# First groups of a hybrid streaming layer: six instead of four on unscaled tokens, operands renewed part by part, low parts on another engine, swish in pieces

## The chip, the cores and the metric

One core of a Trainium2 chip runs one layer of a hybrid trunk (a convolution group and a stick-breaking attention group side by side) on 2048 tokens and 16 meta tokens, in float32. The metric is the device time of one execution in microseconds. The page of the profile names the engines PE (TensorE), DVE (VectorE), ACT (ScalarE), POOL (GpSimd) and SP, which only starts transfers.

## The reference, cut to what matters

```python
u = rms_norm(h, pre_g)                       # per token: u = h * rate * g
proj = u @ w_in                              # 1024 -> 7 x 512 columns
glu_a, glu_b, conv_gate, q, k, v, sb_gate = split(proj)
c = glu_a * sigmoid(glu_b)
c = causal_depthwise_conv(c, conv_w, conv_b) # width 31
c = silu(layer_norm(c, conv_ln_g, conv_ln_b))
c = (c @ w_pw2 + b_pw2) * silu(conv_gate)
s = stick_breaking_attention(q, k, v) * silu(sb_gate)   # 8 heads x 64, strictly causal
h = h + rms_norm(concat[c, s] @ w_out, post_g)
```

The rate of a token is one number, so a product of unscaled tokens with the weights can be multiplied by the rate afterwards. The kernel uses that at its start: the rates take long to get, the products need not wait for them.

## The kernel before, in words

The 2048 tokens go in four chunks of 512 (chunk 0 carries the 16 meta tokens too). Each float32 operand is split into a high part (fp32r) and the rest, the low part: ACT copies the high part, DVE or POOL subtracts it, and each product of two such operands is three matmuls: high by high, high by low, low by high (`mm3`). The normed tokens of a chunk, transposed, are the tiles uh and ul (8 parts of 128 rows each); a weight is a slab of 128x512 numbers, loaded raw (wr), and its two parts lie in w. Two slabs make one group, the 128 output columns of one step of the input projection. Chunk 0 makes each group in two segments of 264 tokens, 24 matmuls each.

Chunk 0 begins with `load_first_in`: it brings the first 512 tokens transposed (ts, in tiles pr), splits them into uh and ul unscaled, and at once brings the same tokens in rows (tok), whose squares ACT sums; POOL makes the rates, PE turns them into a row (`spread`), and DVE scales ts by it (`times`). The groups of glu_b and glu_a (names G_B, G_A; `in_proj`) come first, in pairs j = 0 to 3. Before, pairs 0 and 1 ran on unscaled tokens, with `with_rates` putting the rates on their results; then `again` renewed uh and ul from the scaled ts, all eight parts in a row, and every later group ran on them.

Behind the pairs come the groups of k, v and q, then attention (`attention`) of the chunk, with which the gates, the norm of the convolution (`conv_norm`), the pointwise projection (`conv_out`) and the next chunk's projection are merged. The convolution of 31 taps per 128 channels runs on DVE as 31 operations that add into a bank cv; in chunk 0 all four tiles run there. `conv_norm` transposes the four tiles (acc), takes mean and variance per token, subtracts and multiplies rows that PE makes of them, and applies swish: per tile two operations of ACT and one product of DVE. `conv_parts` splits the result (mixs) for `conv_out`.

The order of all engines is written out by the program before it runs: `Clock` and `Engine` keep a forecast of each engine's time, `when` puts a deferred piece on a list with the operands it needs and a date before which it is not issued, `step` and `merge` pick what comes next. So a new date or a new cost moves instructions on all engines. What is issued stands in that order in each engine's queue, and the chip follows it. Weights pass through two raw buffers (RAWS) and four slabs of parts (WB); `load_raw` starts a load when a raw buffer is free. All instructions of an engine are issued from one line of the helper (L203 before, L206 after), so the profile tells them apart by tiles.

## Time and profile before

| | us |
|---|---|
| median of 3 runs (1358.3 to 1359.58) | 1358.92 |
| the profiled execution | 1360.08 |
| its span | 1357.9 |
| PE busy / DVE / ACT / POOL | 1320.4 / 1003.4 / 738.2 / 650.5 |
| TensorE's granted clock, mean | 0.988 |

In the rows a line reads: start, duration, engine, line of the program, operation, output <- inputs, shape, how many; in brackets the idle time of the engine ahead of it and what ended it. Tiles: T, mm, cv and av are banks of PSUM, all others lie in SBUF or, with wpack, xturn, x and the names on scr, in HBM. A busy PE isn't always at full speed: the granted clock (PEclk) is 1.00 or 0.50 in any short stretch of this profile.

### The profile page before, as it was taken

How to read it: one execution, taken by the hardware profiler on the slowest of the kernel's cores; microseconds unless marked ns; L12 is line 12 of the kernel's file. 1: busy time of each engine (PE TensorE's matmuls, PEld its weight loads, DVE VectorE, ACT ScalarE, POOL GpSimd, SP SyncE). 2: the span in 40 equal slices, each digit the busy share in tenths (PEclk: the TensorE clock that was granted, in tenths of full speed). 3: DMA queues.
4: the chain of work that ended last, by engine and by line, in shares of the span. 5: the costliest groups of instructions: out<-in, count | busy, mean ns of one | idle time of the engine just before them, and what ended most of it. 6: DMA issues, size and time to landing. Idle time of an engine off the chain costs nothing.

```text
span 1357.9 us, 21813 instructions
## 1 busy us (share of the span) xinstructions
PE 1320.4 (97%) x7584; PEld 1133.7 (83%) x7584; DVE 1003.4 (74%) x1417; ACT 738.2 (54%) x1459; POOL 650.5 (48%) x786
## 2 busy tenths in 40 slices
PE   7999989999998999999999999999999999999997
PEld 7898777887788987887779988888877899988797
DVE  4999864898984376995396468896557987898965
ACT  5334465344446545376645446488776657655542
POOL 5444668667466541297841143089886021141300
PEclk8999989999999999999999999999999999999999
DMA  6155968899985994676776597556777545586655
GB/s 223 66 155 179 343 228 291 295 311 319 336 284 176 305 355 139 195 238 214 230 252 185 168 295 263 176 176 216 221 223 240 174 136 179 161 279 215 210 155 179
DMA packets 163757, 304.95 MB, mean 225 GB/s; under 512 B 16688, under 2 KB 71152, under 8 KB 163648
## 3 DMA queue, kind: packets, MB, share of 16 engines
q1 hardware_dynamic: 149344, 253.49, 59.7%
q0 software_dynamic: 14304, 50.08, 9.4%
q8 instruction: 60, 0.98, 0.3%
q14 instruction: 49, 0.40, 0.1%
HBM read 221.85 MB, written 81.66 MB: 224 GB/s over the span
## 4 chain that ended last, share of the span: by engine, by line
PE 80%; DVE 7%; DMA 4%; ACT 3%; issue 3%; POOL 2%; SPq 0%; DVEq 0%; POOLq 0%; ACTq 0%
PE mm L203 51%; PE T L203 20%; PE av L203 8%; DVE cv L203 2%; DMA tok<-x 1%; DVE pr L203 1%; ACT ev L203 1%; DMA wr<-wpack 1%; POOL w L203 1%; DVE tok L203 1%; DVE ul L203 1%; DVE al L203 1%; POOL ev L203 1%; DVE acc L203 1%; DMA wscr<-w 1%
## 5 line engine op out<-in xcount | busy, mean ns | idle before, releaser
L203 PE MATMUL mm<-uh,w 128*128 128x512 f32 (+1 forms) x1664 | 517.9, 373 | 3.9 <-ACT uh L203 3.9
L203 PEld LDWEIGHTS mm<-uh,w 128*128 128x128 f32 x1664 | 302.2, 191 | 52.6 <-ACT uh L203 4.5
L203 DVE TENSOR_TENSOR al<-T,ah 128x512 fp32r<-128x512 f32 (+3 forms) x323 | 193.9, 600 | 164.7 <-ACT ah L203 163.1
L203 PE MATMUL mm<-ul,w 128*128 128x512 f32 (+1 forms) x832 | 307.0, 369 | 1.1 <-DVE ul L203 1.0
L203 DVE TENSOR_TENSOR_SCAN pr<-T,pr,zcol 128x512 f32<-128x512 f32 x192 | 245.0, 1276 | 47.9 <-ACT T L203 42.7
L203 ACT ACTIVATE ah<-T 128x512 fp32r<-128x512 f32 (+3 forms) x323 | 171.4, 531 | 141.9 <-PE T L203 140.4
L203 DVE SCALAR_TENSOR_TENSOR cv<-ct,cp,cv 128x512 f32<-128x512 f32 x319 | 239.2, 750 | 7.4
L203 ACT ACTIVATE T<-T 128x512 f32<-128x512 f32 (+2 forms) x320 | 167.4, 525 | 110.7 <-PE T L203 108.0
L203 POOL TENSOR_TENSOR acc<-acc,pd 128x512 f32<-128x512 f32 x150 | 194.2, 1294 | 44.5 <-ACT pd L203 37.4
L203 POOL TENSOR_TENSOR w<-wr,w 128x512 fp32r<-128x512 f32 x116 | 149.7, 1294 | 103.8 <-ACT w L203 101.0
L203 PE MATMUL T<-kk,q 128*128 128x512 f32 (+2 forms) x640 | 195.1, 387 | 3.0 <-DVE pr L203 2.3
L203 PEld LDWEIGHTS mm<-ul,w 128*128 128x128 f32 x832 | 158.6, 191 | 22.3 <-DVE ul L203 1.7
L203 PE MATMUL T<-ident,pr 128*128 128x128 f32 x1088 | 172.3, 274 | 1.0 <-DVE al L203 0.6
L203 PEld LDWEIGHTS T<-ident,pr 128*128 128x128 f32 x1088 | 133.9, 141 | 32.7 <-DVE pr L203 2.5
L203 DVE TENSOR_TENSOR_SCAN pr<-T,tri 128x128 f32<-128x128 f32 (+3 forms) x128 | 103.9, 815 | 31.9 <-ACT T L203 31.2
L203 PEld LDWEIGHTS T<-kk,q 128*128 128x128 f32 x640 | 106.4, 190 | 19.3 <-DVE pr L203 4.1
L203 PE MATMUL av<-ah,vk 128*128 128x512 f32 (+1 forms) x320 | 117.4, 367 | 0.0
L203 PE MATMUL av<-al,vk 128*128 128x512 f32 (+1 forms) x320 | 117.1, 366 | 0.0
L203 ACT ACTIVATE pd<-ct,cp 128x512 f32<-128x512 f32 x150 | 106.1, 718 | 19.0 <-POOL acc L203 18.1
L203 PE MATMUL mm<-uh,wr 128*128 128x512 f32 x320 | 115.2, 402 | 0.0
L203 ACT ACTIVATE w<-wr 128x512 fp32r<-128x512 f32 x116 | 72.1, 628 | 77.1 <-PE mm L203 35.2
L203 POOL COPY cm<-pr 128x1 f32<-128x1 f32 x120 | 23.7, 200 | 146.7 <-DVE pr L203 145.8
(188 smaller groups left out, 1802.2 us busy)
## 6 DMA issues: line engine op xcount, KB each, us to landing
w<-wscr SPq DMA_DIRECT2D x128, 512.0 KB, 4.1
wscr<-w POOLq DMA_DIRECT2D x76, 512.0 KB, 5.7
wr<-wscr SPq DMA_DIRECT2D x62, 512.0 KB, 4.2
wr<-wpack SPq DMA_DIRECT2D x58, 512.0 KB, 4.4
kk<-kscr SPq DMA_DIRECT2D x80, 256.0 KB, 4.9
vk<-vscr SPq DMA_DIRECT2D x80, 256.0 KB, 3.7
q<-qscr SPq DMA_DIRECT2D x64, 256.0 KB, 5.6
tok<-x SPq DMA_DIRECT2D x16, 512.0 KB, 8.2
```

What stands on the lines that cost most here:

```text
L203: return call(out, *args, **kw)
```

## The change

EARLY_PAIRS = 3: the first three pairs, six groups instead of four, run on unscaled tokens. The renewal of uh and ul is called by `mm3` behind each part's last product in the second segment of the sixth group (`then`), and the seventh group runs its two segments together in banks T, as the first group does. VectorE instead of GpSimd forms the low parts of slabs 0 and 2 to 7, and the raw loads behind these slabs have no date. The first weight load is cut in two, the second half behind the first part of the tokens; the meta tokens' transposed load moves ahead of the tokens; the last 256 tokens in rows are brought behind another weight load. A sigmoid at the very start brings its table in. The scalings of ts get dates, 1.5 us apart. PE's warm-up has 18 transposes instead of 20. In `conv_norm` of every chunk, the swish of tile j is a deferred piece with a date 1.5 us after that of tile j - 1.

```diff
@@ -66,6 +66,9 @@
         for k in range(0, KD, 2):
             yield "w_out", n, OC, k
+EARLY_PAIRS = 3
@@ -517,6 +520,7 @@
                 there.add(key)
             order.append((key, n, kept, save))
     todo_w = deque(order)
+    FIRST = [len(order) - i - 1 for i in (0, 2, 3, 4, 5, 6, 7)]
     whole = [key for key, n, kept, save in order if not kept]
     at = {key: i for i, key in enumerate(slab_keys())}
     todo_raw = deque(zip(whole[::2], whole[1::2]))
@@ -556,12 +560,19 @@
                         lambda: pool.dma_start(place[key], both.bitcast(F32)), [both[:, 1]]
                     )
-                split(raw[:, i], both[:, 0], both[:, 1], then=keep_it if save else None)
+                split(
+                    raw[:, i], both[:, 0], both[:, 1],
+                    dve if len(todo_w) in FIRST else pool,
+                    keep_it if save else None,
+                )
                 raws[0][1] += 1
                 if i:
                     raws.popleft()
                     when(
-                        lambda: load_raw(min(RAWS, len(raws) + 1)), [], date=pe.now + 2.0, tag="wr")
+                        lambda: load_raw(min(RAWS, len(raws) + 1)), [],
+                        date=0.0 if len(todo_w) in FIRST else pe.now + 2.0, tag="wr",
+                    )
             ready.append(
                 (key, [both[:, i].rearrange("p (k n) -> p k n", n=key[2]) for i in range(2)])
             )
@@ -582,7 +593,7 @@
             parts.append(both)
         return parts
-    def mm3(w, mh, ml, nk, cols, last=True, given=None, tag="mm"):
+    def mm3(w, mh, ml, nk, cols, last=True, given=None, tag="mm", then=None):
         pts = None
@@ -604,6 +615,8 @@
                     pe.matmul(pt, h, hi, start=(k == 0), stop=False)
                     pe.matmul(pt, h, lo, start=False, stop=False)
                     pe.matmul(pt, l, hi, start=False, stop=(k == nk - 1))
+                if then:
+                    then(k)
                 if last and (k % 4 == 3 or k == nk - 1):
                     release()
         return pts
@@ -623,8 +636,13 @@
         uh, ul = u_now
-        load_raw(1)
+        raw = T("wr", [P, 2, 4 * P], RAWS)
+        raws.append([raw, 0])
+        a, b = todo_raw.popleft()
+        sp.dma_start(raw[:, 0], wpack[at[a]])
         sp.dma_start(cp, cpack)
+        mt = T("pr", [P, KD, NM], PR)
+        sp.dma_start(mt, xturn[:, :, :NM])
         keep["turned", 0] = 0
         ts = []
         for k in range(KD):
@@ -632,8 +650,7 @@
             sp.dma_start(ts[k], xturn[:, k, NM:])
             when(lambda k=k: part_in(0, k, ts[k], uh, ul), [ts[k], cp])
             if k == 0:
-                mt = T("pr", [P, KD, NM], PR)
-                sp.dma_start(mt, xturn[:, :, :NM])
+                sp.dma_start(raw[:, 1], wpack[at[b]])
         def meta_in():
             hi, lo = uh[:, :, 0:NM], ul[:, :, 0:NM]
@@ -649,17 +666,23 @@
         when(meta_times, [mt, cp])
         load_raw()
-        todo = []
-        for i in range(NTB // 2):
+        measured = []
+        def fetch(i):
             t = tok()
             for b in range(2):
                 tb = 2 * i + b
                 sp.dma_start(t[:, b], x[tb * P : (tb + 1) * P, :])
-                todo.append((t[:, b], tb))
-        m = T("q2", [P, D], 2)[:NM]
-        sp.dma_start(m, meta)
-        todo.append((m, NTB))
-        measured = []
+                when(lambda b=b, tb=tb: measure(t[:, b], tb), [t[:, b]], tag="ev")
+        def fetch_meta():
+            m = T("q2", [P, D], 2)[:NM]
+            sp.dma_start(m, meta)
+            when(lambda: measure(m, NTB), [m], tag="ev")
+        fetch(0)
+        fetch_meta()
+        when(lambda: fetch(1), [], date=7.5)
         def measure(t, tb):
             n = t.shape[0]
@@ -668,11 +691,8 @@
                 junk[:n], t, AF.Square, scale=D ** -0.5, accum_out=squares[:n, tb : tb + 1]
             )
             measured.append(tb)
-            if len(measured) == len(todo):
+            if len(measured) == NTB + 1:
                 when(rates, [squares], [rate0])
-        for t, tb in todo:
-            when(lambda a=(t, tb): measure(*a), [t], tag="ev")
         def rates():
             pool.tensor_scalar(squares, squares, 1e-6, None, op0=ALU.add)
@@ -698,7 +718,9 @@
             for go in waiting:
                 go()
             for k in range(KD):
-                when(lambda k=k: times(k, pt), [ts[k], pt], [ts[k]])
+                when(
+                    lambda k=k: times(k, pt), [ts[k], pt], [ts[k]], date=pe.now + 3.0 + 1.5 * k
+                )
             dve.tensor_tensor(
                 mt, mt, row[:, :NM].unsqueeze(1).to_broadcast([P, KD, NM]), op=ALU.mult
             )
@@ -709,22 +731,21 @@
             dve.tensor_tensor(ts[k], ts[k], rates, op=ALU.mult)
             scaled.append(k)
-        def again():
-            yield need(given=lambda: len(scaled) == KD and "first" in keep)
-            keep["turned", 0] = 0
-            keep["normed"] = True
-            meta_in()
-            for k in range(KD):
-                when(lambda k=k: part_in(0, k, ts[k], uh, ul), [ts[k]])
-        return again()
+        def once_more(k):
+            if k == 0:
+                keep["turned", 0] = 0
+                when(meta_in, [mt], date=pe.now)
+            when(lambda: part_in(0, k, ts[k], uh, ul), [ts[k]], date=pe.now)
+        keep["scaled"] = lambda: "row" in keep and len(scaled) == KD
+        keep["once more"] = once_more
     def warm():
         pt = PT("T", [P, TC])
-        for _ in range(20):
+        for _ in range(18):
             pe.transpose(pt[:, :P], ident, ident)
     waiting = []
@@ -795,22 +816,24 @@
     def proj(c, g, evac, with_meta):
         yield need(given=lambda: ("turned", c) in keep and (c or "meta" in keep))
-        first = G_B, G_A, G_B + 1, G_A + 1
-        if c == 0 and g == first[-1]:
+        first = [n + j for j in range(EARLY_PAIRS) for n in (G_B, G_A)]
+        if c == 0 and g == first[3]:
             yield need(given=lambda: "row" in keep)
-        if c == 0 and g not in first:
-            keep["first"] = True
-            yield need(given=lambda: "normed" in keep)
         w = weights(w_in, g * P)
         uh, ul = u_now
         cols = segs(c, with_meta)
-        for part in [cols] if c == 0 and g == first[0] else [[a] for a in cols]:
+        for part in [cols] if c == 0 and g in (G_B, G_B + EARLY_PAIRS) else [[a] for a in cols]:
+            then = None
+            if c == 0 and g == first[-1] and part[-1] == cols[-1]:
+                yield need(given=keep["scaled"])
+                then = keep["once more"]
             pts = yield from mm3(
                 w, lambda k: uh[:, k], lambda k: ul[:, k], KD, part, part[-1] == cols[-1],
                 (lambda k: k < keep["turned", c]) if keep["turned", c] < KD else None,
-                "T" if c == 0 and g in first[1:3] else "mm",
+                "T" if c == 0 and g in (*first[1:3], G_B + EARLY_PAIRS) else "mm", then,
             )
             for pt, (o, n) in zip(pts, part):
                 evac(pt, o, n)
@@ -876,11 +899,11 @@
                 def go():
                     dve.tensor_tensor(t, pt, row[:, o : o + n], op=ALU.mult)
                     act.activation(t, t, AF.Sigmoid)
-                    if j < 2:
+                    if j < EARLY_PAIRS:
                         pool.tensor_tensor(t, t, row[:, o : o + n], op=ALU.mult)
-                if c == 0 and j < 2:
+                if c == 0 and j < EARLY_PAIRS:
                     with_rates(go)
                 else:
                     act.activation(t, pt, AF.Sigmoid)
@@ -1093,13 +1116,16 @@
                     lambda j=j, i=i: apply(j, i), [rows[i], accs[j]], [accs[j]]
                 )
         yield need(given=lambda: len(done) == 2 * NJ)
-        for j in range(NJ):
+        def swish(j):
             g, b = lng[:, j : j + 1], lnb[:, j : j + 1]
             sg, y = ev()[:, :TC], accs[j]
             act.activation(sg, y, AF.Sigmoid, scale=g, bias=b)
             act.activation(y, y, AF.Identity, scale=g, bias=b)
+            when(lambda: dve.tensor_tensor(y, y, sg, op=ALU.mult), [y, sg], [y])
+        for j in range(NJ):
             when(
-                lambda y=y, sg=sg: dve.tensor_tensor(y, y, sg, op=ALU.mult), [y, sg], [y]
+                lambda j=j: swish(j), [accs[j]], [accs[j]], date=pe.now + 1.5 * j, tag="ev"
             )
         keep["normed", c] = True
@@ -1802,10 +1828,12 @@
     ):
         new_u()
         warm()
-        once_more = load_first_in()
+        load_first_in()
+        act.activation(rate0[:, 0:1], zcol, AF.Sigmoid)
         prepare()
         clear()
-        spent = [merge(iter(()), either(in_proj(0), once_more), iter(()), [(1, 1)])]
+        spent = [merge(iter(()), in_proj(0), iter(()), [(1, 1)])]
         for half in range(2):
             in_us(4.0 + 6 * half, lambda half=half: load_in(1, half))
         for c in range(NCH):
```

What the order of instructions shows at three places. First VectorE around the renewal: ul is the low part of the tokens, pr the tokens, cv the taps of the convolution, ct what glu gives. Before:

```order
L203 SCALAR_TENSOR_TENSOR cv_418<-ct0_92,cp_71,cv_418 128x512 x3
L203 TENSOR_TENSOR ct1_93<-mm_420,ehl_379 128x264
L203 SCALAR_TENSOR_TENSOR cv_418<-ct0_92,cp_71,cv_418 128x512 x3
L203 TENSOR_TENSOR ct1_93<-mm_451,ehl_379 128x264
L203 SCALAR_TENSOR_TENSOR cv_418<-ct0_92,cp_71,cv_418 128x512
L203 TENSOR_TENSOR ul_105<-pr_132,uh_104 128x8x16
L203 SCALAR_TENSOR_TENSOR ul_105<-pr_130,cp_71,uh_104 128x512
L203 SCALAR_TENSOR_TENSOR ul_105<-pr_134,cp_71,uh_104 128x512
...
L203 SCALAR_TENSOR_TENSOR ul_105<-pr_146,cp_71,uh_104 128x512
L203 SCALAR_TENSOR_TENSOR cv_418<-ct0_92,cp_71,cv_418 128x512 x9
```

Now:

```order
L206 SCALAR_TENSOR_TENSOR cv_446<-ct0_92,cp_71,cv_446 128x512 x4
L206 TENSOR_TENSOR ehl_509<-mm_516,row_81 128x264
L206 SCALAR_TENSOR_TENSOR cv_446<-ct0_92,cp_71,cv_446 128x512 x3
L206 TENSOR_TENSOR ct2_94<-mm_552,ehl_509 128x264
L206 TENSOR_TENSOR ul_105<-pr_128,uh_104 128x8x16
L206 SCALAR_TENSOR_TENSOR ul_105<-pr_130,cp_71,uh_104 128x512
...
L206 SCALAR_TENSOR_TENSOR ul_105<-pr_141,cp_71,uh_104 128x512
L206 TENSOR_TENSOR ct2_94<-mm_582,ehl_509 128x264
L206 SCALAR_TENSOR_TENSOR ul_105<-pr_143,cp_71,uh_104 128x512
L206 SCALAR_TENSOR_TENSOR ul_105<-pr_145,cp_71,uh_104 128x512
L206 SCALAR_TENSOR_TENSOR cv_446<-ct0_92,cp_71,cv_446 128x512 x8
L206 TENSOR_TENSOR ct3_95<-mm_699,ehl_693 128x264
```

The renewal (rows ul) stood ahead of the third pair's results (ct2); it now stands among them, ct2_94<-mm_582 being the second segment of the sixth group.

Second VectorE at the end of chunk 0's last convolution (acc_1501 before, acc_1599 now; pr are attention's scans, ev an attention gate, mixc a convolution gate, bst the norm's statistics). Before:

```order
L203 SCALAR_TENSOR_TENSOR pr_1772<-T_1768,tri_74 128x128
L203 SCALAR_TENSOR_TENSOR cv_1502<-ct3_95,cp_71,cv_1502 128x512
L203 SCALAR_TENSOR_TENSOR acc_1501<-ct3_95,cp_71,cv_1502 128x512
L203 SCALAR_TENSOR_TENSOR pr_1788<-T_1784,tri_74 128x256
L203 TENSOR_TENSOR ev_1797<-mm_1742,ev_1797 128x512
L203 TENSOR_TENSOR al_1812<-T_1805,ah_1810 128x512
L203 BN_STATS bst_1823<-T_1818 128x6
L203 BN_AGGR bmv_1825<-bst_1823 128x2
L203 BN_STATS bst_1832<-T_1827 128x6
```

Now:

```order
L206 SCALAR_TENSOR_TENSOR pr_1970<-T_1966,tri_74 128x128
L206 SCALAR_TENSOR_TENSOR cv_1600<-ct3_95,cp_71,cv_1600 128x512
L206 TENSOR_SCALAR tok_1748<-tok_1748,st2_1981 128x1024
L206 SCALAR_TENSOR_TENSOR cv_1600<-ct3_95,cp_71,cv_1600 128x512 x2
L206 TENSOR_TENSOR mixc_1944<-mm_1954,mixc_1944 128x512
L206 TENSOR_TENSOR al_2016<-T_2012,ah_2014 128x128
L206 SCALAR_TENSOR_TENSOR pr_2022<-T_2018,tri_74 128x256
L206 SCALAR_TENSOR_TENSOR cv_1600<-ct3_95,cp_71,cv_1600 128x512 x4
L206 SCALAR_TENSOR_TENSOR acc_1599<-ct3_95,cp_71,cv_1600 128x512
L206 TENSOR_TENSOR al_2063<-T_2056,ah_2061 128x512
L206 TENSOR_TENSOR mixc_1945<-mm_2024,mixc_1945 128x512
L206 BN_STATS bst_2083<-T_2078 128x6
```

Ahead of the last tap now stand a scaling of the next chunk's tokens (tok) and a convolution gate (mixc); before, an attention gate (ev_1797) still stood behind it, and the convolution gates further back.

Third ScalarE at the norm of chunk 1: ev<-acc and acc<-acc are a tile's swish, ev,sq and tok<-mm an output bank's square sums and its evacuation, w a weight's high part. Before:

```order
L203 ACTIVATE ev_4524<-acc_2654,cp_71 128x512
L203 ACTIVATE acc_2654<-acc_2654,cp_71 128x512
L203 ACTIVATE ev_4527<-acc_2969,cp_71 128x512
L203 ACTIVATE acc_2969<-acc_2969,cp_71 128x512
L203 ACTIVATE ev_4530<-acc_3324,cp_71 128x512
L203 ACTIVATE acc_3324<-acc_3324,cp_71 128x512
L203 ACTIVATE ev_4533<-acc_3727,cp_71 128x512
L203 ACTIVATE acc_3727<-acc_3727,cp_71 128x512
L203 ACTIVATE ev_4549,sq_4315<-mm_4453 128x256
L203 ACTIVATE ev_4552,sq_4315<-mm_4453 128x256
L203 ACTIVATE tok_4314<-mm_4453 128x2x256
L203 ACTIVATE w_4548<-wr_4329 128x512
```

Now:

```order
L206 ACTIVATE ev_4528<-acc_2658,cp_71 128x512
L206 ACTIVATE acc_2658<-acc_2658,cp_71 128x512
L206 ACTIVATE ev_4544,sq_4319<-mm_4457 128x256
L206 ACTIVATE ev_4546,sq_4319<-mm_4457 128x256
L206 ACTIVATE tok_4318<-mm_4457 128x2x256
L206 ACTIVATE ev_4552<-acc_2973,cp_71 128x512
L206 ACTIVATE acc_2973<-acc_2973,cp_71 128x512
L206 ACTIVATE w_4543<-wr_4333 128x512
L206 ACTIVATE ah_4578<-T_4574 128x384
L206 ACTIVATE ev_4582<-acc_3328,cp_71 128x512
L206 ACTIVATE acc_3328<-acc_3328,cp_71 128x512
L206 ACTIVATE T_4585<-T_4585 128x512
```

The evacuation now stands behind the first tile's swish instead of the fourth's, the weight's high part behind the second's.

## The prediction

> **What bounds the kernel now.** I read the page first, then the timeline of TensorE at its longest waits, then the granted clock in stretches laid around them.
>
> ```profile
> span 1357.9 us, 21813 instructions
> PE 1320.4 (97%) x7584; PEld 1133.7 (83%) x7584; DVE 1003.4 (74%) x1417; ACT 738.2 (54%) x1459; POOL 650.5 (48%) x786
> ```
>
> TensorE (PE) is busy for 97% of the span. A change that takes no product away, as this one, can gain only what PE now idles, and what it runs at a lowered clock. Its longest waits, in its timeline (start, us, the wait ahead and its releaser in brackets):
>
> ```profile
> 8.61 0.39 PE L203 MATMUL mm<-uh,w 128*128 128x264 f32 x1 [2.26 <-ACT uh L203]
> 28.43 0.81 PE L203 MATMUL T<-uh,w 128*128 128x264 f32 x2 [3.17 <-POOL w L203]
> 42.91 0.39 PE L203 MATMUL mm<-uh,w 128*128 128x264 f32 x1 [1.61 <-ACT uh L203]
> 44.26 0.40 PE L203 MATMUL mm<-ul,w 128*128 128x264 f32 x1 [0.96 <-DVE ul L203]
> 175.32 0.48 PE L203 MATMUL T<-ident,st 128*128 128x128 f32 x1 [2.99 <-POOL st L203]
> 214.28 2.44 PE L203 MATMUL T<-ident,tok 128*128 128x128 f32 x12 [1.73 <-DVE ul L203]
> 423.50 0.39 PE L203 MATMUL mm<-w,mixs 128*128 128x256 f32 x1 [1.84 <-ACT w L203]
> 425.56 1.72 PE L203 MATMUL mm<-w,mixs 128*128 128x256 f32 x11 [1.67 <-POOL w L203]
> ```
>
> Three places: the first groups, the convolution norm of chunk 0 with what follows it, and that of chunk 1. A wait costs twice, as the granted clock in the stretches behind them shows (PEclk, then DMA share and GB/s):
>
> ```profile
> 10.37:13.78 3.41, 3.41 (x18) 3.41 (x17) 3.41 (x6) 3.41 (x7) 0.27 (x1) 0.50 1.04 408
> 27.44:34.27 6.83, 5.84 (x26) 5.85 (x27) 6.20 (x11) 0.59 (x2) 3.56 (x4) 0.50 0.45 154
> 44.51:47.92 3.41, 3.41 (x16) 3.28 (x16) 3.41 (x6) 2.64 (x5) 0.00 (x0) 0.50 0.40 154
> 48.90:101.20 52.30, 52.30 (x429) 52.30 (x430) 48.99 (x72) 16.09 (x32) 23.51 (x21) 1.00 0.43 123
> 174.21:181.04 6.83, 5.72 (x15) 4.56 (x16) 3.04 (x6) 1.35 (x4) 6.05 (x12) 0.50 1.01 277
> 215.17:218.58 3.41, 3.41 (x15) 3.19 (x14) 3.22 (x6) 3.00 (x6) 0.79 (x3) 0.50 0.98 317
> 426.80:430.20 3.40, 3.40 (x16) 3.10 (x16) 0.09 (x1) 2.77 (x9) 0.30 (x2) 0.50 0.94 316
> 500.00:520.00 20.00, 18.07 (x95) 14.46 (x93) 15.78 (x21) 13.83 (x27) 10.06 (x14) 1.00 0.83 278
> ```
>
> Half the stretch is lost at clock 0.50: 1.7 us of 3.41, 3.4 of 6.83. Not every wait does it: the last row holds 1.9 us of idle PE and keeps 1.00. At full clock a product of 264 columns takes 52.30 / 429 = 0.122 us.
>
> **The change part by part: the first groups (A).** In the order PE now meets the transposes of the rates 18 products into the third group, so all before it is free only up to the moment the rates exist. What makes them:
>
> ```profile
> 18.31 1.06 ACT L203 ACTIVATE ev<-tok 128x1024 bf16<-128x1024 f32 x1 [0.52 <-DMA tok<-x]
> 19.36 1.04 ACT L203 ACTIVATE ev<-q 16x1024 bf16<-16x1024 f32 x1
> 21.01 1.21 POOL L203 TENSOR_TENSOR rate<-squares,nhalf 128x5 f32<-128x5 f32 x1
> 23.13 0.39 PE L203 MATMUL T<-uh,w 128*128 128x264 f32 x1
> 23.92 1.28 ACT L203 ACT_TABLE_LOAD   x1
> ```
>
> The last tokens land at 18.31; SP's queue now holds one weight load more ahead of them (512 KB; at the 408 GB/s above 1.3 us), so 19.6. (That load waits in the queue for the first load's buffer, and the last tokens behind it, but the buffer is free near 8 us, long before the DMA engines are.) Before, the last square (19.36) was followed by the next product at 23.13, 3.8 us later; now 19.6 + 3.8 = 23.4. Starting earlier (operands after half a weight load: I count PE's first product near 6.0 instead of 8.61, the first group ending near 13 instead of 16.5) brings PE to that place near 21, where it waits some 2 us: the early start is worth only the products done by then. If the rates came sooner, it would be worth up to 2 us more. Behind the transposes stand 6 + 24 products of the third group, 144 of the next three and 48 of the seventh, 222 x 0.122 = 27.1 us. ACT's table load (1.28) goes to the start, where ACT waits for weights anyway.
>
> Three waits are to be priced there. The weights' low parts: POOL made them behind the rates, and PE waited 3.17. Now VectorE (DVE) makes seven of the first eight, none behind POOL's power; rows of DVE with two operands in SBUF, of its idling there, and of POOL's low parts:
>
> ```profile
> L203 DVE TENSOR_TENSOR acc<-acc,ev 128x512 f32<-128x512 f32 x4 | 5.2, 1308 | 0.0
> 23.93 0.77 DVE L203 TENSOR_TENSOR ehl<-mm,row 128x264 f32<-128x264 f32 x2 [10.00 <-ACT row L203]
> 43.46 5.38 DVE L203 SCALAR_TENSOR_TENSOR ul<-pr,cp,uh 128x512 fp32r<-128x512 f32 x8
> 40.72 2.68 POOL L203 TENSOR_TENSOR w<-wr,w 128x512 fp32r<-128x512 f32 x2 [1.02 <-ACT w L203]
> ```
>
> So 0.67 to 1.31 us each on DVE against 1.34 on POOL. Five or six lie in the 10 us that DVE idled before 23.93; the eighth slab's stands behind six small operations that wait for the rates, and PE reaches it about 0.5 us early: 0.5 (0 to 1.3). The renewal: before, all eight parts stood behind the last product (1.61 + 0.96 us); now each stands behind its own last product in the second half of the sixth group.
>
> ```profile
> 8.59 0.29 DVE L203 TENSOR_TENSOR ul<-pr,uh 128x128 fp32r<-128x128 f32 x1 [0.38 <-ACT uh L203]
> 42.49 1.05 DVE L203 TENSOR_TENSOR ul<-pr,uh 128x128 fp32r<-128x128 f32 x1
> ```
>
> A part costs DVE 5.38 / 8 = 0.67 (row 43.46), and PE takes six products of it, 0.73: PE is the slower, once the first part is there. DVE stands behind three taps then (0.75 each), so the first part is late by about 0.5; two low parts of POOL run beside it. The two rows, 1.05 us beside POOL's low parts of 40.72 and 0.29 without, say what that can do. I take 1.0 in all (0 to 5). Sum: 23.4 + 27.1 + 0.5 + 1.0 = 52.0 for the end of the seventh group. Before it ended at 48.90 + 120 x 0.122 = 63.5. **A = 11.5** (7 to 13; a half clock behind the wait for the rates would take 1.7).
>
> "SBUF — State Buffer" in the Trainium skill (Who interferes with whom) says a VectorE operation with two SBUF inputs and a GpSimd operation that reads SBUF exclude each other for the whole instruction. The 1.05 and the 1308 above agree. By it alone the change moves low parts to the engine that then blocks; it is the third rival.
>
> **The norm of chunk 0 (B).** DVE does not get this gain: it is full from 34 us on.
>
> ```profile
> L203 DVE SCALAR_TENSOR_TENSOR cv<-ct,cp,cv 128x512 f32<-128x512 f32 x116 | 87.3, 753 | 3.2
> 126.80 0.80 DVE L203 TENSOR_SCALAR cv<-ct,cp 128x512 f32<-128x512 f32 x1
> 158.35 1.88 PE L203 MATMUL T<-ident,acc 128*128 128x128 f32 x12
> 172.39 1.15 ACT L203 ACTIVATE w<-wr 128x512 fp32r<-128x512 f32 x2 [1.47 <-DMA wr<-wpack]
> 202.54 1.27 POOL L203 TENSOR_TENSOR mixs<-acc,mixs 128x512 fp32r<-128x512 f32 x1
> 227.18 1.56 PE L203 MATMUL mm<-mixs,w 128*128 128x512 f32 x6
> 228.58 0.40 PE L203 MATMUL mm<-uh,w 128*128 128x512 f32 x1
> ```
>
> The first row is DVE from 33 to 160 us. In the new order the fourth convolution starts two Q groups later as PE counts (24 products each, of (228.58 - 227.18) / 6 = 0.233 us: 5.6 a group, 11 in all), that is at the same 126.8 by the clock. Behind its start DVE now has 31 taps (24 us) and 24 other operations up to the last tap (scans, gates, scalings of tokens, some 17 us by their rows), so it ends near 168; before, PE took its result at 158.35. PE has four more gate groups and pieces of attention in front of the transposes of acc, and comes there near 172: it waits for nothing yet. Then the norm's chain, 6 + 6 products of gates between its steps, brings PE to the end of the gates near 189. From there DVE has eight parts of ul (0.74), four products acc x ev, four results of the pointwise projection, and scans and low parts of one and a half heads, in all some 17 to 20 us; PE has 10 us of its own there and then 36 products of 0.233. So the first product of chunk 1's projection, at 228.58 before, comes near 210: 18.5 earlier, 7 of it beyond A, since the waits of 2.99 and 1.73 and the half clocks of 6.83 and 3.41 us (5.1 lost) are replaced by about 3 us of waiting for banks that DVE frees. But transfers:
>
> ```profile
> 140.00:160.00 20.00, 19.87 (x99) 15.89 (x97) 17.68 (x26) 8.92 (x19) 11.44 (x19) 1.00 1.00 352
> 160.00:183.00 23.00, 19.49 (x87) 15.66 (x85) 13.81 (x26) 9.39 (x20) 15.03 (x28) 0.85 1.04 339
> ```
>
> The DMA engines are full there, 352 x 20 + 339 x 23 = 14.8 MB, and the same bytes now meet gate groups that follow one another more closely. I take 3 us off: **B = 4** (-10 to 10).
>
> **The norm of chunk 1 (C).** ACT's eight swish operations stood in one row, 415.39 to 421.73, with the square sums, the copies to tok and a weight's high part behind them:
>
> ```profile
> 415.39 0.80 ACT L203 ACTIVATE ev<-acc,cp 128x512 f32<-128x512 f32 x1
> 420.91 0.82 ACT L203 ACTIVATE acc<-acc,cp 128x512 f32<-128x512 f32 x1
> ```
>
> PE's 1.84 and 1.67 and the half clock after them (1.7) are that, over 5 us in all. Now four pairs are spread, the evacuation behind the first pair, the weight behind the second. The weight's part comes two pairs or 3.2 us earlier, less the evacuation's time, against 3.5 us of waiting. **C = 4** (0 to 5.2). In chunks 2 and 3 PE does not wait at their norms: 0. Between the places PE's order is the same as before, and PE full: the gains carry through. Two transposes fewer at the start: 0, they lie ahead of the first operands.
>
> Sum: 11.5 + 4 + 4 = 19.5. The profiled execution took 1360.08 (span 1357.9); less 19.5 is 1340.6, and the median of the runs stands 1.16 below the profiled one: **1339.4 us**.
>
> **The rivals.** First: all waits of B and C go and transfers cost nothing: 11.5 + 10 + 5, less 26.5, 1332. For it: 183 to 207 has little traffic; against: DVE. Second: the norm's chain of chunk 0 is the bound. Before it took from the transposes of acc (158.35) to the end of the last low part (202.54 + 1.27) 45.5 us; if it takes them again from 172, and 10 us of pointwise projection after it, the projection of chunk 1 starts at 227, 1.5 earlier, and the total is 1.5 + 4: 1353. For it: DVE is later than now; against: in those 45 us POOL's last rate stood behind a low part whose weight landed late (172.39), and the new order has the rates in one run. Third, that the renewal isn't hidden: each part takes 1.31 instead of 0.67, 5 us later, and a half clock of 1.7: 1346. Against it: only two operations of POOL stand beside it. Fourth, transfers: the gates run no faster than their 14.8 MB, and B is -3: 1346. On the other side stands the same mechanism at a higher price: each of the eight gate groups waits for its weights behind saves of earlier ones. From 2.3 us a group on (8 x 2.3 = 18.4, over A and C with the 2.7 us of 0.2%) the kernel is slower: 1362 or more. The trace has one such delay, the load that reached ACT at 172.39, and it cost one wait of 2.99.
>
> "TensorE: Matmul & The Clock Gate" in the Trainium skill (Part 1, the HAM clock gate) says that the clock is judged in free-running windows of 3.413 us and falls after an idle window. By it no wait that is left here, all under 3 us, would lower the clock; the trace agrees on the length (3.41) and not on the rest: 1.73 us of idle lowered it, 1.9 did not.
>
> **How the numbers follow.** The forecast with its own range (1335 to 1345) 0.55; first rival 0.12; second 0.12; third and fourth 0.07 and 0.09; the slower one 0.03, and 0.02 for nothing. Range 1331 to 1351. A run of this kernel tells about 0.2% (2.7 us) from no change: faster 0.94, same 0.03, slower 0.03.
>
> **What would show it.** A: the seventh group's last product near 52 us; a wait of 1 to 2.5 us before the transposes of the rates; none over 0.7 at the renewal; two half-clock stretches fewer before 50 us. B: the waits on st at 175 gone, PE's waits between 185 and 200 on DVE or ul, and 14 to 19 us ahead at the projection of chunk 1. C: no wait on w over 1 us near 405. Wrong would be: waits on wr or w between 130 and 190 (transfers), a gain under 9 us by 60 us (the renewal or the rates), or a projection of chunk 1 that starts after 222 (the chain).

## The result, and the profile after

The changed kernel took **1348.77 us** (median of five runs, 1346.53 to 1351.98) beside 1358.92 (five runs, 1357.62 to 1361.82) for the kernel before: a ratio of 0.9928, 95% interval 0.991 to 0.9945. It is faster by 10 us where 19.5 were forecast: inside the range, 9.4 us above the forecast. Two later sets of runs on other chips gave 0.9949 (0.9932 to 0.9966) and 0.9955 (0.994 to 0.997); over the three sets the gain is 6 to 10 us.

The profiled execution took 1347.43. Its page begins:

```profile
span 1345.7 us, 21801 instructions
PE 1313.2 (98%) x7582; PEld 1127.2 (84%) x7582; DVE 1008.8 (75%) x1426; ACT 736.4 (55%) x1459; POOL 643.0 (48%) x781
```

Its timeline of TensorE at the places of the forecast (start, us, the wait ahead and its releaser in brackets; of the two rows without brackets, the first is where PE reaches the norm's transposes of acc, forecast near 172, and the second the first product of chunk 1's projection, at 228.58 before):

```profile
6.92 0.59 PE L206 MATMUL mm<-uh,w 128*128 128x264 f32 x1 [0.99 <-ACT uh L206]
50.95 0.39 PE L206 MATMUL T<-ul,w 128*128 128x264 f32 x1 [1.01 <-DVE ul L206]
52.64 0.39 PE L206 MATMUL T<-ul,w 128*128 128x264 f32 x1 [0.69 <-DVE ul L206]
162.95 0.50 PE L206 MATMUL mm<-uh,w 128*128 128x512 f32 x1 [1.95 <-ACT w L206]
164.31 0.85 PE L206 MATMUL mm<-uh,w 128*128 128x512 f32 x2 [0.62 <-POOL w L206]
178.53 0.60 PE L206 MATMUL T<-ident,acc 128*128 128x128 f32 x4
200.93 0.80 PE L206 MATMUL T<-kk,q 128*128 128x256 f32 x2 [4.54 <-DVE ul L206]
220.86 0.40 PE L206 MATMUL mm<-uh,w 128*128 128x512 f32 x1
415.62 1.56 PE L206 MATMUL mm<-w,mixs 128*128 128x256 f32 x11 [1.28 <-POOL w L206]
492.32 0.50 PE L206 MATMUL av<-ah,vk 128*128 128x512 f32 x1 [1.20 <-ACT ev L206]
```

The first groups did what was forecast. The convolution norm of chunk 0 did not: in place of the old waits at 175 and 214 stand new ones at 163 and 201. The lead over the kernel before, taken at one and the same product in both traces, tells it by stage; the times at the head of the columns are those of the kernel before. The second and third rows are later profiles of the unchanged kernel (spans 1352.7 and 1354.3). The differences between neighbouring columns are A, B, C and a remainder, and all of them stand against one profile of before. The first profile is of an execution 1.3 us below the median of its set, the second and third are of executions 1.2 and 3.5 us above theirs, so the rows differ more than the three sets of runs do.

| execution of the kernel after | behind the first groups (107 us) | in chunk 1's projection (268) | behind chunk 1's norm (576) | end |
|---|---|---|---|---|
| first (this page) | 10.4 | 8.4 | 11.0 | 12.2 |
| second | 9.3 | 8.1 | 4.9 | 5.2 |
| third | 9.2 | 5.9 | 3.9 | 3.6 |
| forecast | 11.5 | 15.5 | 19.5 | 19.5 |

**Where B went.** VectorE and ScalarE (ACT) in the timeline of the kernel after, ahead of the end of the fourth convolution (acc<-ct is its last tap):

```profile
159.52 1.06 ACT L206 ACTIVATE ev<-tok 128x1024 bf16<-128x1024 f32 x1 [4.57 <-DMA tok<-x]
...
161.18 1.22 DVE L206 TENSOR_TENSOR_SCAN pr<-T,tri 128x512 f32<-128x512 f32 x1 [5.51 <-ACT T L206]
162.26 1.15 ACT L206 ACTIVATE w<-wr 128x512 fp32r<-128x512 f32 x2 [1.11 <-DMA wr<-wpack]
...
172.60 0.69 DVE L206 TENSOR_TENSOR mixc<-mm,mixc 128x512 f32<-128x512 f32 x1 [1.64 <-ACT mixc L206]
...
177.15 0.75 DVE L206 SCALAR_TENSOR_TENSOR acc<-ct,cp,cv 128x512 f32<-128x512 f32 x1
```

ACT stood 4.57 us at the square sum of chunk 1's tokens, whose load had not landed, and 1.11 us more at a weight. Behind the square sum stood the evacuation of scores that VectorE's scan waits for; VectorE stood 5.51 us with taps behind the scan. Between 127.4 and 177.9, from the last tap of the third convolution to the last tap of the fourth, VectorE was busy 40.2 of 50.5 us:

```profile
127.40:177.90 50.50, 47.93 (x216) 38.13 (x215) 40.19 (x59) 22.20 (x45) 29.63 (x46) 0.97 1.01 341
```

(columns: length, PE, PEld, DVE, ACT, POOL, granted clock, DMA share, GB/s). The fourth convolution's own part of this, from its first tap at 129.0, is 38.8 us of work and 10.1 of waiting: 5.5 at that scan and 3.6 in smaller waits for ACT, the longest 1.64. The forecast's count of VectorE's work (24 + 17 us from 126.8) was about right; it left no room for the waiting. The DMA engines are full all along, 1.01.

The kernel before has the same stand at the same load, 10 us behind the end of its fourth convolution, where no tap stood behind it:

```profile
168.78 1.06 ACT L203 ACTIVATE ev<-tok 128x1024 bf16<-128x1024 f32 x1 [4.49 <-DMA tok<-x]
```

Then the end of the chain, in ACT's rows ahead of the wait of 4.54:

```profile
193.02 0.64 ACT L206 ACTIVATE w<-wr 128x512 fp32r<-128x512 f32 x1 [2.10 <-DMA wr<-wpack]
...
199.42 1.82 ACT L206 ACTIVATE uh<-T,cp 128x512 fp32r<-128x512 f32 x3
```

Between the two stand three of the four swish pairs, so the first evacuation of chunk 1's operands (uh) comes at 199.4, its low part (ul) at 200.1, and PE, whose next bank that operation frees, waits from 196.4 to 200.9 and runs at half clock for 6.83 us from 198.9 on. The row at 193.02 is a stand at a transfer too, ahead of the first swish: ACT waited 2.10 us there for a weight, and 3.57 and 2.35 in the two later profiles.

### The profile page after: what moved, and what is told of

Same layout as the page of the kernel before. It is cut to its first block, busy times and chain, and to the rows that moved or that the text cites. A ratio compares the mean times of both kernels' runs of the same rounds, so it can differ in the third digit from the quotient of the medians.

```text
span 1345.7 us, 21801 instructions
## 1 busy us (share of the span) xinstructions
PE 1313.2 (98%) x7582; PEld 1127.2 (84%) x7582; DVE 1008.8 (75%) x1426; ACT 736.4 (55%) x1459; POOL 643.0 (48%) x781
## 4 chain that ended last, share of the span: by engine, by line
PE 82%; DVE 5%; ACT 4%; DMA 3%; POOL 2%; issue 2%; SPq 0%; DVEq 0%; POOLq 0%; ACTq 0%
PE mm L206 53%; PE T L206 21%; PE av L206 9%; DMA wr<-wpack 1%; ACT ev L206 1%; DVE cv L206 1%; DVE ul L206 1%; POOL w L206 1%; DMA tok<-x 1%; POOL ev L206 1%; DMA wr<-wscr 1%; DVE pr L206 1%; DVE tok L206 1%; DVE al L206 0%; ACT uh L206 0%
## 5 line engine op out<-in xcount | busy, mean ns | idle before, releaser
L206 PE MATMUL mm<-uh,w 128*128 128x512 f32 (+1 forms) x1632 | 509.7, 373 | 3.6 <-ACT w L206 1.9
L206 PEld LDWEIGHTS mm<-uh,w 128*128 128x128 f32 x1632 | 295.5, 189 | 52.7 <-ACT w L206 2.4
L206 PE MATMUL mm<-ul,w 128*128 128x512 f32 (+1 forms) x816 | 301.0, 369 | 0.2 <-DVE ul L206 0.2
L206 ACT ACTIVATE ah<-T 128x512 fp32r<-128x512 f32 (+3 forms) x323 | 171.5, 531 | 153.0 <-PE T L206 151.5
L206 POOL TENSOR_TENSOR w<-wr,w 128x512 fp32r<-128x512 f32 x109 | 141.3, 1299 | 88.5 <-ACT w L206 86.5
L206 PEld LDWEIGHTS mm<-ul,w 128*128 128x128 f32 x816 | 154.7, 190 | 21.1 <-DVE ul L206 0.9
```

The costliest lines, as they stand in the source:

```text
L206: return call(out, *args, **kw)
```

## The experiments

All ratios are to the kernel before, which ran beside each kernel on the same chip, with their 95% interval. None of these kernels leaves out a part of the computation.

**The swish in one row again.** The kernel after without its last edit:

```diff
-        def swish(j):
+        for j in range(NJ):
...
-        for j in range(NJ):
             when(
-                lambda j=j: swish(j), [accs[j]], [accs[j]], date=pe.now + 1.5 * j, tag="ev"
+                lambda y=y, sg=sg: dve.tensor_tensor(y, y, sg, op=ALU.mult), [y, sg], [y]
```

> The kernel after, with the eight swish operations of each chunk in one row on ACT again, as before. Theory: the pieces are worth their 4 us in chunk 1 only (ACT's queue ahead of a weight's high part), so the waits of PE near 405 to 415 come back (3 us of waiting and 1.7 of a half clock) and the total is 1348.8 + 4 = 1352 to 1354; in chunk 0 the row stands where six of its eight operations stood already, ahead of the evacuations of uh, so the lead over the kernel before at the first product of chunk 1's projection stays at 6 to 9 us. Rival: the pieces themselves cost chunk 0 its place (the wait of 4.5 us at 201); then that lead grows to 11 or more here, and the total stays within 1.5 of 1348.8 or falls. Second rival: the gain at chunk 1 comes from the other edits; then nothing changes at 405 to 415.

Measured: 0.9993 (0.9981 to 1.0006), 1357.18 us: the whole gain is gone, 5 to 9 us by the three ratios of the kernel after, where 4 were expected. Waits of PE:

```profile
207.53 0.79 PE L206 MATMUL T<-kk,q 128*128 128x256 f32 x2 [8.71 <-DVE ul L206]
420.12 0.38 PE L206 MATMUL mm<-w,mixs 128*128 128x256 f32 x1 [1.82 <-ACT w L206]
422.64 2.51 PE L206 MATMUL mm<-w,mixs 128*128 128x256 f32 x11 [2.14 <-POOL w L206]
```

At chunk 1 the old waits are back, as expected (3.96 us and a half clock). At chunk 0, where I had expected no difference, the wait is 8.71 us (4.54, 6.00 and 4.78 in the three profiles of the kernel after) and the half clock there lasts 10.2 us instead of 6.8: with all eight operations ahead of it the evacuation of uh comes at 204.2 instead of 199.4, 2.5 us of which this execution had already lost in the first groups. From 107 to 268 us its lead falls by 4.5 us, in the kernel after by 2.0, 1.2 and 3.3. The rival that the pieces hurt chunk 0 falls. The expectation held that six of the eight operations stand ahead anyway, and so counted no difference; the last two, and what they push behind them, cost 1 to 3 us by these traces.

**The pieces alone**, in the kernel before (the same edit the other way):

> The kernel before with one edit of the change alone: the swish of the convolution norm in pieces. Theory: it is worth what it was worth in the kernel after at chunk 1, 4 us (3 to 5), and nothing at chunk 0, where the evacuations of uh stand well behind: 1354 to 1356. Rival: in chunk 0 it disturbs ACT's order: its second wait at 214 grows, and the total is 1358 or more.

Measured: 0.9992 (0.9977 to 1.0008), no difference. Taken at the same products, the lead over the kernel before is −1.05 us at 412 (this execution had one more half clock near 8), +2.2 at 435, 0.7 at 445, 0.1 at 471, and −2.1 behind this wait, which the kernel before does not have:

```profile
500.25 1.06 ACT L203 ACTIVATE ev<-tok 128x1024 bf16<-128x1024 f32 x1 [2.57 <-DMA tok<-x]
...
504.56 0.50 PE L203 MATMUL av<-ah,vk 128*128 128x512 f32 x1 [1.93 <-ACT ev L203]
```

ACT again stands at a square sum for the next chunk's tokens, now of chunk 2, with the evacuation of av behind it: what PE gains at the norm it loses again, half of it at the next load and half before it, between 435 and 471, in small waits (the longest 0.64 us). So C is there at its place, 3.3 us, and is gone 70 us later. The same wait stands in all three profiles of the kernel after, 1.20, 3.35 and 2.18 us at 492 to 498; in the second and third a half clock follows, which makes their C negative in the table.

**The low parts on POOL again**, and with them the old dates of the raw loads; the rest of the change stays:

```diff
-    FIRST = [len(order) - i - 1 for i in (0, 2, 3, 4, 5, 6, 7)]
+    FIRST = []
```

> The kernel after, with the first seven weights' low parts on POOL again and their loads given at the dates of before; the early start, six groups and the renewal part by part stay. Theory: POOL's low parts (1.34 us each) stand behind the rates again and PE waits for one as before (3.2 us and half clocks of 3.4): the seventh group ends 3 to 8 us later than in the kernel after, and the total is 1352 to 1356. Rival: the order of the groups alone is the gain of the first 60 us, and the low parts' engine changes nothing: 1347 to 1350, lead over the kernel before at 60 us still 10. The other side of that rival: VectorE's low parts delay the convolution, and the total falls below 1346.

Measured: 0.9975 (0.9961 to 0.9988), 1354.46 us. In the first 60 us it costs little: one wait of 0.78 us (row below) instead of the 3.17 of before, and a lead of 8.5 behind the first groups against 9.2 to 10.4. The other waits of this trace lie where the low parts of the first slabs have no business: at 203 (4.81 us), 212 (0.69) and 497 (2.03, with a half clock). The later profiles of the kernel after have the first and the last of them in like size (6.00 and 3.35, 4.78 and 2.18), and the interval meets those of its later two sets (up to 0.9966 and 0.997). So the expected total was met, but a loss of that size isn't shown; the expected cause, POOL's low parts behind the rates, is worth about 1 us.

```profile
35.40 0.36 PE L206 MATMUL mm<-uh,w 128*128 128x264 f32 x1 [0.78 <-ACT w L206]
```

**Four groups instead of six** (EARLY_PAIRS = 2):

> The kernel after with four groups on tokens without rates instead of six; the early start, low parts on VectorE and the renewal part by part stay. Theory: the rates exist near 23 and the eight scalings and the renewal follow; four groups hold 192 products, 24 us behind a first product at 6.9, so PE comes to the renewal near 33 with the second halves, where scalings and low parts are not far enough ahead: it waits 3 to 5 us and a half clock of 1.7 to 3.4, total 1352 to 1356. Rival: the gain of the first 60 us is the early start and the low parts; the lead there stays 10 and the total within 1.5 of 1348.8.

Measured: 0.9948 (0.9933 to 0.9963), 1350.94 us, no difference from the kernel after that these runs can tell. Two waits of PE:

```profile
37.59 0.59 PE L206 MATMUL T<-ul,w 128*128 128x264 f32 x1 [2.65 <-DVE ul L206]
201.65 0.50 PE L206 MATMUL T<-kk,q 128*128 128x256 f32 x2 [2.23 <-DVE ul L206]
```

The renewal costs nearly what was expected there, 2.65 us and a stretch of 3.4 us at half clock; the lead behind the first groups is 7.5 instead of 10.4, so the rival's unchanged lead falls, and the expected total of 1352 to 1356 falls too. But chunk 1's projection starts at 218.2, earlier than in the kernel after (220.9), since the wait at 201 is 2.23 instead of 4.54 and lowers no clock. The planner's order in chunk 0 differs too, so this is no undoing of one edit alone; in this trace 3 us of lead less at 107 are not seen at 220.

**The renewal in a row** behind the sixth group's last product:

```diff
-                then = keep["once more"]
+                again = True
...
+            if again:
+                for k in range(KD):
+                    keep["once more"](k)
```

> The kernel after, but the operands' renewal stands in one row behind the sixth group's last product instead of part by part behind each part's last product. Theory: eight parts of 0.67 us on VectorE beside the next group's products of 0.73 us a part, with the first part open: PE waits as the kernel before did at its renewal (1.61 + 0.96 us, and a half clock of 1.7), where the kernel after waited 1.01 + 0.69; total 1349.5 to 1351.5. Rival: the next group's products wait for nothing that matters, and the order of the renewal is worth nothing: 1348 to 1349.3.

Measured: 0.9967 (0.9943 to 0.9992), 1353.71 us, beside 0.9949 for the kernel after on the same chip: the intervals overlap. Its trace has the waits that the theory gave, 1.59 and 0.96 us at 47 to 49 and a half clock of 3.41, and a lead of 8.1 behind the first groups. The renewal part by part is worth 1 to 2 us there by these traces; that the total keeps it isn't shown.

**Chunk 1's token loads later:**

```diff
-            in_us(4.0 + 6 * half, lambda half=half: load_in(1, half))
+            in_us(16.0 + 14 * half, lambda half=half: load_in(1, half))
```

> The kernel after with the two loads of chunk 1's tokens given 12 and 20 us later (16 and 30 us behind the end of chunk 0's Q, gate and K groups in the planner's count, instead of 4 and 10); the square sums on ACT move back with them. Theory (transfers ahead of ACT): between 155 and 161 ACT stood 4.57 us at a square sum for these tokens, with an evacuation of scores and a weight's high part queued behind it; VectorE stood 5.5 us, the convolution ended at 177.9 instead of 168, and PE waited 2.6 us near 163. With the square sums behind those, the waits near 163 go, the last tap ends 3 to 6 us earlier and the total is 1344 to 1347 on a chip where the kernel after has 1348.8. Rival: the tokens come too late for the projection of chunk 1, and PE waits at the transposes of tok near 205 for longer than the 4.5 us of now: 1350 or more. Second rival: the DMA engines are the bound whatever the order, and the same bytes make another transfer late: 1348 to 1350.

Measured: **0.9907** (0.9887 to 0.9926), 1346.83 us beside 1353.34 for the kernel after on the same chip, and so faster than both kernels. PE's timeline:

```profile
172.27 0.76 PE L206 MATMUL T<-ident,acc 128*128 128x128 f32 x5 [0.63 <-DVE acc L206]
193.12 0.50 PE L206 MATMUL av<-ah,vk 128*128 128x512 f32 x1 [1.00 <-ACT ev L206]
197.00 1.11 PE L206 MATMUL T<-ident,pr 128*128 128x128 f32 x4 [1.96 <-DVE ul L206]
215.39 0.40 PE L206 MATMUL mm<-uh,w 128*128 128x512 f32 x1
```

No wait over 0.6 us stands between 118 and 172; the last tap starts at 171.5, 5.7 us earlier; chunk 1's projection starts at 215.4 instead of 220.9, a lead of 13.2 there. The weight at which ACT stood until 162.26 in the kernel after lands earlier:

```profile
156.78 0.63 ACT L206 ACTIVATE w<-wr 128x512 fp32r<-128x512 f32 x1 [4.53 <-DMA wr<-wpack]
```

PE's order is that of the kernel after up to 175 us, and between 107 and 175 this kernel gains 4.5 us on it; behind that the order differs too. The first rival, that the tokens then come too late, falls, and so does the second.

**The same loads earlier** (0.0 + 2 * half):

> The kernel after with the two loads of chunk 1's tokens given 4 and 8 us earlier (0 and 2 us instead of 4 and 10). Theory (transfers ahead of ACT): the tokens' third and fourth parts land before ACT comes to their square sums, so its wait of 4.57 us near 157 shrinks below 1, but the weight's loads stand behind them in SP's queue and one weight is still late near 160: 1345 to 1348. Rival: the engines are full, and what the tokens gain the weights lose: PE waits more on w between 150 and 165, 1349 or more.

Measured: 0.9948 (0.9933 to 0.9963), 1353.09 us, the kernel after's own 0.9949 on that chip, so the expected gain did not come. ACT's longest wait for tokens shrinks to 2.52 us. PE's wait at 163 is replaced by 0.83 and 0.62 us at 158, for the weight before that one; the wait at 203.5 is 6.25. ACT's rows at two weights (the first was taken at 145.47 in the kernel after, the second is that of 193.02):

```profile
157.49 1.15 ACT L206 ACTIVATE w<-wr 128x512 fp32r<-128x512 f32 x2 [2.65 <-DMA wr<-wpack]
...
195.65 0.63 ACT L206 ACTIVATE w<-wr 128x512 fp32r<-128x512 f32 x1 [4.39 <-DMA wr<-wpack]
```

The tokens are four loads of 512 KB; asked for sooner, they still stand ahead of the weights. With less waiting near 163 and no half clock there, this execution gains 2.5 us on the first profile of the kernel after between 107 and 175, and has lost them again by 221: ACT stands longer at the weight ahead of the swish. The second profile of the kernel after does the same (2.2 us gained by 175, 1.5 lost by 221, with 3.57 us at that weight).

**The loads where they are, the square sums later.** Did the bytes cost the time, or ACT standing at them?

```diff
-        when(measure, [t], tag="ev")
+        when(measure, [t], date=pe.now + 18.0, tag="ev")
```

> The kernel after with every token load where it is, but the square sums of the next chunk's tokens given to ACT 18 us behind their load's issue instead of as soon as the planner counts them landed: ACT's evacuation of scores at 155 and that of av at 490 now stand ahead of them. Theory (ACT's queue): what cost the time was the engine standing at a square sum with other work behind it, not the bytes; ACT's waits on tok (10 to 12 us in all) shrink under 4, VectorE's stand of 5.5 us near 157 goes, the last tap of the fourth convolution ends 3 to 5 us earlier than the 176 to 178 of the kernel after, the waits on av near 490 go, and the ratio to before is 0.989 to 0.992, as with the loads themselves moved. Rival (transfers): the weight lands at the same time as before whatever ACT does, so the wait near 163 stays, and the ratio is 0.993 to 0.995, that of the kernel after.

Measured: 1.0023 (1.0012 to 1.0034), 1361.47 us: slower than the kernel before, and my theory for this run fell. ACT no longer waits for tokens near 160, and waits as long for the weight, with PE behind it as before:

```profile
164.82 1.15 ACT L206 ACTIVATE w<-wr 128x512 fp32r<-128x512 f32 x2 [4.62 <-DMA wr<-wpack]
...
165.50 0.50 PE L206 MATMUL mm<-uh,w 128*128 128x512 f32 x1 [1.83 <-ACT w L206]
```

The last tap starts at 179.2, no earlier than in the kernel after (176 to 179). So near 160 it is the transfers: the weight is taken at 164.82 instead of 162.26, in an execution that was already 2.3 us behind at 107, so it lands no earlier for what ACT does meanwhile, and fewer bytes ahead of it, as with the later loads, do help. That it became slower has another place: the lead is 6.8 us at 510, 3.7 at 608, 4.2 at 830 and −2.5 at 1095. The planner, given the later square sums, orders PE's work from 510 to 580 and near 840 differently; the next two runs show what happens there. The wait for av near 490 is gone, as expected, but one of 1.53 us for a later av stands at 516.

**Both** (chunk 1's loads later, the square sums of chunks 2 and 3 later), and the same with loads 8 and 12 us later instead of 12 and 20:

> The kernel after with chunk 1's token loads 12 and 20 us later, and in the later chunks the square sums 18 us behind their load's issue. Theory: the gain of the later loads (6 us) and the waits on av near 490 (2.3 us and a half clock of 1.7) add up: ratio to before 0.987 to 0.990. Rival: a wait at 490 only moves into the next group, and the ratio is that of the later loads alone, 0.9907.

> The same, with the token loads 8 and 12 us later than in the kernel after instead of 12 and 20. Theory: if PE's remaining waits near 193 to 199 come from tokens that are scaled late, this takes 1 to 3 us more off: ratio 0.986 to 0.989. Rival: the third square sum meets its load in ACT's queue again, with the evacuation of scores behind it: 0.991 to 0.993.

Measured: 0.997 (0.996 to 0.998) and 0.9981 (0.997 to 0.9991), 1354.92 and 1354.98 us. In chunk 1's projection the first has the lead of the later loads alone (13.1 us), the second 10.7: both expectations fall behind that, in the later chunks. The wait for av is gone near 490 in both, and one of 1.5 us stands at 508 and 511, as the rival of the first had it; but both are slower than that rival too. At the second place, the run with chunk 1's loads alone and then the first of these two, from their tables by stretches:

```profile
820.00:840.00 20.00, 20.00 (x120) 17.24 (x120) 17.54 (x25) 13.96 (x27) 6.45 (x8) 1.00 0.53 160
840.00:860.00 20.00, 20.00 (x98) 16.42 (x97) 14.34 (x19) 7.85 (x16) 2.28 (x4) 1.00 0.57 172
```

```profile
820.00:840.00 20.00, 17.34 (x91) 13.48 (x89) 15.16 (x21) 11.38 (x23) 5.97 (x9) 1.00 0.52 170
840.00:860.00 20.00, 18.54 (x97) 14.47 (x96) 14.27 (x20) 10.54 (x19) 2.46 (x5) 1.00 0.39 111
```

PE idles 4.1 us of 40 and starts 188 operations instead of 218; the lead falls by 6.6 us there (11.9 at 830, 5.3 at 880). In the trace stand scores, scans and their transposes of one head after the other, with waits of 1.33, 0.71 and 0.64 us between them and no projection products of the next chunk to fill them, as the run with the later loads alone has there; these need the tokens that are now scaled later. So in the later chunks the square sums are better early.

**The kernel after once more**, on two other chips:

> The kernel after, unchanged, once more. Theory on the clock: a stretch of 3.41 us runs at half clock when PE idled at least half (1.7 us) of the window of 3.41 us before it; the windows' position against the program differs from one execution to the next, so that a wait of 1 to 3 us lowers the clock in one execution and not in another. Then this profile has the same waits (near 7, 51, 163 and 201) within 0.5 us, but half-clock stretches in other places (behind 7 or 51, or none at 165), and the time differs from 1347.4 by 1.7 us for each. Rival: the stretches belong to the waits, and stand behind 163 and 201 again and nowhere else; the time differs by less than 1 us.

> The kernel after, unchanged, beside the three others on the same chip: 0.9925 to 0.995 of before, the waits near 7, 51, 163, 201 and 490 as in its first two profiles, and half-clock stretches behind those of them that put 1.7 us of idling into one window of 3.41.

Measured: 0.9949 (0.9932 to 0.9966), 1353.34 us, and 0.9955 (0.994 to 0.997), 1352.52. The waits are in the same places, not within 0.5 us throughout: 1.42, 1.33, 6.00 and 3.35 us near 7, 163, 201 and 495 in the first of the two, and 1.06, 1.77, 4.78 and 2.18 in the second, which also has the wait for the rates (1.11 at 24.5). The half clocks are in other places: behind 7, 201 and 497; behind 164, 201 and 499. The last section shows what decides that.

## Why the prediction was right or wrong

**The first groups (A): right.** 10.4, 9.3 and 9.2 us against 11.5 (7 to 13). PE reaches the transposes of the rates at 23.3, 25.5 and 24.5 in the three profiles (forecast 23.4), and the seventh group ends at 53.5 in the first (forecast 52.0). PE's first product came at 6.9 to 7.2, not 6.0. The forecast that the early start is worth only what is done by the time the rates arrive holds: in the second profile a half clock of 6.83 us lies behind the first products, and its lead is only 1.1 lower. The renewal took 1.01 + 0.69 us, forecast 1.0 in all. The third rival (renewal not hidden) falls. Of the wait for the rates, forecast at 1 to 2.5 us, one profile of three shows 1.11. What the forecast did not separate: low parts on VectorE are worth about 1 us by the one trace without them, not the 3.17 of the wait that they replaced.

**The norm of chunk 0 (B): wrong, −2.0, −1.2 and −3.3 instead of +4.** The step that failed is "so it ends near 168": the working summed VectorE's operations and let it never wait. The work was 38.8 us where 41 were summed; VectorE stood 10.1 us more, over half of it since ACT stood at a load, and the last tap ended at 177.9. PE, held up near 163 by the same late transfers (2.6 us, and 1.7 of a half clock), reached the transposes of acc at 178.5 instead of 172, 0.6 us behind that tap and without a wait; so which of the two delays alone would have set this time isn't shown. The second half of the same step is "I take 3 us off" for the transfers: a flat allowance, which no row prices, and which the waits at 163 with their half clock already exceed. From there "about 3 us of waiting for banks" near 189 became 4.54 to 6.0 us and a half clock of 3.4 us lost. The transfers were the **fourth rival** (B = −3, 1346): B came out near that, and the sign set down for it, a wait on w between 130 and 190, is the wait at 163. I gave it 0.09 because the 14.8 MB seemed to fit; the rows of before had already shown the case, ACT's 1.47 at 172.39 behind a load of 512 KB and the 4.49 at 168.78, which the working left out. What is shown for it: moving 2 MB of tokens behind the weights, with their square sums, gives 5.5 us at chunk 1's projection; moving ACT's work without the bytes gives nothing. That ACT's stand at the weight of 193 then holds the swish is read from the traces; no run moves that load alone.

The second rival (the chain from the transposes of acc, 45.5 us) falls: it had 55 us from the transposes of acc to chunk 1's projection (172 to 227), the forecast 38, and 42.4 passed (178.5 to 220.9). Half of its idea holds: in the twelve traces with the new start this passage took 42 to 48 us, whether it began at 170 or at 181, so the forecast's 38 was too short by 4 and what PE is late at the transposes it is late at the projection. The slower rival fell: no gate group but the one at 163 waits.

**The norm of chunk 1 (C): right at its place, not kept.** At 423 us the lead had grown by 4 (8.4 to 12.4); at 576 2.6 of it were left in the first profile, and nothing in the two others. "Between the places PE's order is the same, and PE full: the gains carry through" is the step that failed: a load that lands at its own time, ACT's square sum in front of the evacuation of av, took it back in part. At its place 1.28 to 2.08 us of waiting on w are left, where the forecast had none over 1. With the pieces alone, half of the loss came before that load, in smaller waits that no run takes apart. The pieces did more than forecast at chunk 0, where I costed them at nothing: without them 1 to 3 us more are lost there.

**The sum.** 10.4 − 2.0 + 2.6 + 1.2 (to the end) = 12.2 in the first profile; 5.2 and 3.6 in the others. That the total fell inside the range is in part luck: of the three terms only A came as forecast, the range was 20 us wide, and its upper end asks for a gain of 7.9 us, which the first set has (10.2) and the two later ones have not (6.8 and 6.4). The price of a wait was mis-sized too: the working counted half clocks by where they stood in one profile. In the second profile three stretches of 3.4 us are half clock that the first does not have, while one of the first is missing; in the third two are added. Each loses 1.7 us.

## What to carry to other kernels

A lead won at the start is kept only up to the next thing that comes at its own time: a load, a norm's chain on another engine. Before adding gains along a program, look in each later stage for the engine that stands at a transfer with other work queued behind it, here ScalarE's square sums, and ask when that transfer lands, not how long the work takes. If the DMA engines are full, order the loads by who is first waited for; moving the waiting engine's work alone only changes the name of what it waits for.

## What the runs showed of the hardware

TensorE's clock. Cut each profile into windows of 3.413 us that fit the recorded half-clock stretches (these start at whole multiples of 3.413 us from each other within a trace, and at another offset in each execution). In 14 profiles, of the windows at full clock in which PE idled 1.76 us or more, 40 of 40 were followed by a half clock. Of those with 1.0 to 1.70 us it was 3 of about 70, and none below that; between 1.70 and 1.76 it was 6 of 10. Half a window is 1.71 us. Three pairs of windows by the tables of stretches, of the first profile of the kernel after, then of the second, then of the kernel before (idle is length less the first number; the clock is the third number from the end):

```profile
161.36:164.77 3.41, 1.20 (x4) 0.72 (x5) 2.75 (x5) 2.51 (x5) 2.03 (x4) 1.00 1.08 364
164.77:168.18 3.41, 3.41 (x11) 2.74 (x10) 3.38 (x7) 1.85 (x5) 3.25 (x7) 0.50 0.90 204
```

```profile
162.42:165.83 3.41, 1.81 (x7) 1.20 (x8) 2.15 (x5) 3.12 (x7) 2.42 (x3) 1.00 1.08 349
165.83:169.24 3.41, 3.41 (x17) 2.83 (x16) 3.38 (x7) 1.03 (x3) 3.25 (x7) 1.00 0.99 228
```

```profile
419.97:423.38 3.41, 1.70 (x15) 1.50 (x13) 0.00 (x0) 3.38 (x10) 0.36 (x1) 1.00 0.33 123
423.38:426.79 3.41, 1.61 (x11) 1.41 (x12) 2.93 (x4) 0.94 (x3) 3.11 (x4) 1.00 0.11 7
```

At the same wait near 163 PE idled 2.21 us of its window in the first execution and 1.60 in the second; only the first lost the clock. In the kernel before 1.71 us kept it and 1.80, one window on, lost it (the row at 426.80 in the prediction). Of the windows at half clock, 18 of 18 with 0.6 us or more of idle PE were followed by another at half, and one of 41 with less. So a wait of g us, longer than half a window and shorter than a whole one, lowers the clock when half a window of it falls into one window: by these lengths, as an estimate, with a chance of g / 3.41. The 1.9 us that kept the clock in the kernel before, which the prediction quotes, lay in two windows, 0.70 and 1.22.

The Trainium skill's page "TensorE: Matmul & The Clock Gate" (Part 1, the HAM clock gate) has the free-running window of 3.413 us, and the offsets that differ by execution agree with it. Its state table has the clock fall after an idle window; here half an idle window was enough.
